# Expert weights in seven 1 MB buffers, with products in groups of four loads

## The chip, the cores and the metric

The kernel runs on one NeuronCore of a Trainium2 chip, in one launch. The metric is the device time of the program in microseconds (us), as the median of its runs. TensorE (PE) multiplies matrices, VectorE (DVE), ScalarE (ACT) and GpSimd (POOL) work element by element, and SyncE (SP) issues nearly all transfers from HBM into on-chip memory. Each engine works through its own instructions in a fixed order and waits at semaphores for the others.

## The reference

Two blocks follow each other on 256 tokens of width 1024, all in fp32. The first block has two kinds of attention, a cross attention and a layer of experts; the second has two layers with modulation, feed-forward networks and mixers, and it carries a second stream of 256 context rows beside the tokens. What matters here is the expert layer of the first block:

```python
group_logits = t @ w_group + b_group                 # 4 groups of 8 experts
g_sel = argmax(group_logits); g_w = softmax(group_logits)[g_sel]
top_vals, top_idx = lax.top_k(expert logits of g_sel, 2)
weights = softmax(top_vals) * g_w
# for each of 32 experts, on the tokens sent to it
hb = silu(xb @ w_gate[e]) * (xb @ w_up[e])           # w_gate, w_up: 1024 x 512
out[token] += (hb @ w_down[e]) * weight              # w_down: 512 x 1024
return x + out
```

All 32 experts' weights are read whatever the routing: 32 x 3 x 2 MB is 192 MB of the 617 MB that the program moves. The context stream of the second block does not depend on the first block, so its work can be done at any time before the tokens need it.

## The kernel before

Two instruction streams are woven into one program. The stream *fore* (tiles named f...) does the first block, the experts (`moe`) and then the tokens of the second block. The stream *back* (tiles b...) does the context rows: `late` and `context` give its parts. A scheduler merges both at build time into one fixed order per engine. It goes by priorities, a start and a slope per section in the table `SEG`, and by its own model of when each instruction can start. On each engine a stream's instructions keep their own order (`link`).

A weight load of fore is one transfer of 128 x 2048 fp32, 1 MB, into a buffer of the tag `raw`, of which fore has 4; a load of back is 128 x 1024, 512 KB, into one of 5. All of them are issued by SP in one order (`load`): a load waits until the last reader of its buffer is done, and everything behind it on SP waits too. For most products ACT rounds the weights (tile `sph`), POOL for back or DVE for fore takes the rest (`spl`), and PE multiplies both parts; a back buffer comes free when POOL is done with it. Expert weights go to PE as they are, so an expert buffer comes free when PE has finished its products.

The experts are worked off in eight groups of four experts. `experts_in` goes over 8 chunks of the model width: per chunk it issues two loads, one of gate and one of up weights, and then multiplies the up load and the gate load, four products of 32 columns each, one per expert. `experts_out` does the same with 4 x 2 loads of the down weights. So a group of experts takes 24 loads, in pairs, and all eight take 192. After the fifth group `spill` handles one more block of 32 tokens with six loads in the same four buffers. A loop for further spills follows the last group; in this run it is not entered. `gather` brings the tokens of the next two groups, `combine` adds results to the residual. Behind `moe` the token stage of the second block begins.

Of the kernel before, what the change touches and what calls it, by code (L numbers as in the profile page):

```python
# [20 lines left out]
KC = 8  # L21
# [18 lines left out]
class X2:  # L40


    def __init__(self, h, l, both=None):
        self.h, self.l, self.both = h, l, both
# [27 lines left out]
class Stream:  # L72
    def __init__(self, K, es, name, bufs, ps_bufs, unit):
        self.K, self.name, self.bufs = K, name, bufs
        self.pool = es.enter_context(K.tc.tile_pool(name=name, bufs=1))
        self.pp = es.enter_context(K.tc.tile_pool(name=name + "p", bufs=ps_bufs, space=PSUM))
        self.n = self.ada = self.lows = 0
        self.sq = None
        self.pool_low = LOW.get(name)
        self.unit = unit  # L80
        self.chain, self.side = {}, {}
        self.seg(0, 1)

    def seg(self, start, slope):

        self.start, self.slope, self.done = start, slope, 0.0
# [8 lines left out]

    def t(self, tag, shape, dt=F32):
        self.n += 1
        return self.pool.tile(shape, dt, tag=tag, bufs=self.bufs[tag], name=f"{self.name}{tag}{self.n}")

    def parts(self, n=T):  # L100

# [56 lines left out]
class Kern:  # L158
    def __init__(self, tc, I, dbg=None):
        self.tc, self.real, self.I, self.dbg = tc, tc.nc, I, dbg  # L160
        self.nc = Engines(self, tc.nc)
        self.cur = self.stream = None
        self.p0 = tc.cur_priority
        self.after = {}

    def link(self, key, r):
        if self.cur is None:
            return
        for prev in (self.cur.get(key), self.after.pop(key, None)):
            if prev is None:  # L170
                continue
            self.tc.add_manual_dep(
                r.ins, prev, mybir.DependencyInfo(mybir.DependencyClass.NoSync, mybir.DependencyReason.DATA),
                reason="stream order")
        self.cur[key] = r.ins.name
# [20 lines left out]
    def pair(self, S, src):  # L196

        if S.unit == 2048:
            raw = self.load(S, src)
            return raw[:, :1024], raw[:, 1024:]  # L200
        return [self.load(S, src[:, i * 1024:(i + 1) * 1024]) for i in range(2)]

    def misc(self, S, tag, shape, src, dt=F32):
        t = S.t(tag, shape, dt)
        self.real.gpsimd.dma_start(t, src)
        return t
# [824 lines left out]
    def moe(self, S):  # L1031
# [7 lines left out]
        xx = S.t("xx", [128, 2, 2, 1024], F32R)  # L1039
# [12 lines left out]
        def ct(n):  # L1052
            used[0] += n
            return scratch[:, used[0] - n:used[0]]
# [23 lines left out]
        dg = ct(8).rearrange("p (b n) -> p b n", b=2)  # L1078
# [58 lines left out]
        def onehot(base, n, b, shift=None):  # L1137
            d = S.t("c", [128, 2])
            if shift is None:
                ts(d, dest[:, :, b], -float(base), None, op0=OP.add)  # L1140
            else:
                tt(d, dest[:, :, b], shift.to_broadcast([128, 2]), op=OP.subtract)
            o, f = S.t("k1", [128, n], F32R), S.t("k1", [128, n])
            ts(f, iota[:, :n], d[:, 0:1], None, op0=OP.is_equal)
            stt(o, iota[:, :n], d[:, 1:2], f, op0=OP.is_equal, op1=OP.add)
            return o
# [13 lines left out]
        def combine(py, s):  # L1160

            o, ws = s
            Yh, Yl = S.t("k4", [128, 1024], F32R), S.t("k4", [128, 1024], F32R)
            for i in range(2):
                q = slice(i * 512, (i + 1) * 512)
                self.split_to(Yh[:, q], Yl[:, q], py[i], ws)
            for d in range(0, KC, 2):
                p = S.ps([128, 2, T])
                for i in range(2):
                    q = slice((d + i) * 128, (d + i + 1) * 128)  # L1170
                    self.mm(p[:, i], Yh[:, q], o, True, False)
                    self.mm(p[:, i], Yl[:, q], o, False, True)
                nc.vector.tensor_tensor(xres[:, d:d + 2], xres[:, d:d + 2], p, op=OP.add)

        wg, wu, wd = I["w_eg"], I["w_eu"], I["w_ed"]

        def gather(pair):
            P = [onehot(256 * pair, 256, b) for b in range(2)]
            xg = [S.t("k4", [128, 4, T]) for _ in range(2)]
            for k in range(0, KC, 2):  # L1180
                p = S.ps([128, 2, T])
                for i in range(2):
                    q = slice((k + i) * 128, (k + i + 1) * 128)
                    for b in range(2):
                        self.mm(p[:, i], hm[b][0][:, q], P[b], b == 0, False)
                        self.mm(p[:, i], hm[b][1][:, q], P[b], False, b == 1)
                nc.scalar.activation(xg[k // 4][:, k % 4:k % 4 + 2], p, AF.Copy)
            return xg

        def experts_in(grp, xg):  # L1190
            g = grp % 2
            pg = [S.ps([128, 512]) for _ in range(2)]
            for k in range(KC):
                raws = [self.load(S, wt[grp, k]) for wt in (wg, wu)]
                for s in (1, 0):
                    for j in range(4):
                        self.mm(pg[s][32 * j:32 * j + 32],
                                xg[k // 4][:, k % 4, g * 128 + 32 * j:g * 128 + 32 * j + 32],
                                raws[s][:, j * 512:(j + 1) * 512], k == 0, k == KC - 1)
            a = self.gated(S, pg[0], 512)  # L1200
            stt(a, a, 0.5, pg[1], op0=OP.mult, op1=OP.mult)
            return a

        def experts_out(grp, a):
            pt = S.ps([128, 512])
            for c in range(4):
                nc.tensor.transpose(pt[:, c * 128:(c + 1) * 128], a[:, c * 128:(c + 1) * 128], self.ident)
            hT = S.t("k2", [128, 4, 128])
            nc.scalar.activation(hT.rearrange("p a b -> p (a b)"), pt, AF.Copy)
            py = [S.ps([128, 512]) for _ in range(2)]  # L1210
            for c in range(4):
                raws = [self.load(S, wd[grp, 2 * c + i]) for i in range(2)]
                for i in (1, 0):
                    for j in range(4):
                        self.mm(py[i][32 * j:32 * j + 32], hT[:, c, 32 * j:32 * j + 32],
                                raws[i][:, j * 512:(j + 1) * 512], c == 0, c == 3)
            slot = S.t("c", [128, 1])
            ts(slot, self.cst[:, C_PCOL:C_PCOL + 1], 128.0 * grp, None, op0=OP.add)
            combine(py, scatter(slot))

        xg = gather(0)

        ta, tb = S.t("k2", [128, 16, 32]), S.t("k2", [128, 16, 32])
# [69 lines left out]
        for grp in range(8):  # L1293
            a = experts_in(grp, xg)
            if grp % 2 == 1 and grp < 7:
                xg = gather(grp // 2 + 1)
            experts_out(grp, a)
            if grp == SPILL:
                spill(sync.value_load(ti[0:1, 0:1], min_val=0, max_val=7),
                      sync.value_load(ti[0:1, 16:17], min_val=0, max_val=3))  # L1300

        self.moe_load = S.chain["sync"]

        n_more = self.real.values_load(ti[0:1, 32:33], min_val=0, max_val=15)
        keep_chain, self.cur = self.cur, None
        with tc.For_i(0, n_more) as it:
# [516 lines left out]


SPILL = 4
DEFER = 0
PLAN = {-1: 'rrr', 0: 'r', 6: 'r', 8: 'raak'}
PLAN_N = 32
CUT = ((0, 9, 9, 9, 9), (0, 3, 3, 3, 3))
FORE = dict(raw=4, sph=3, spl=3, xx=1, k1=6, k2=4, k4=6, c=16, q1=4, dg=2, ld=1, dst=6, wg=2, gc=5, c72=1, rope=1)  # L1830
BACK = dict(raw=5, sph=3, spl=3, xh=1, xl=1, k1=4, k2=4, k4=3, c=16, q1=2, wg=1, gc=4, c72=1)
SEG = dict(c1b=(1150, 2), first=(-5000, 1), ada=(0, 0), c0a=(300, 1.25), c0b=(530, 1.3), c0c=(680, 1.3), ada1=(950, 3), c1a=(1050, 4.8),
           route=(-5000, 1), moe=(365, 2.6), tok=(1050, 1.38))
# [3 lines left out]
def kernel(ctx: ExitStack, tc: tile.TileContext, I, out, dbg=None, stop=None):  # L1837
    K = Kern(tc, I, dbg)
    nc = K.nc
    fore = Stream(K, ctx, "f", FORE, 5, 2048)  # L1840
    back = Stream(K, ctx, "b", BACK, 3, 1024)
    K.dram = ctx.enter_context(tc.tile_pool(name="dram", bufs=1, space=bass.MemoryType.DRAM))
    K.setup(fore, ctx)

    def context():
# [113 lines left out]
    for c in range(KC):  # L1959
        nc.vector.scalar_tensor_tensor(x[:, c], x[:, c], K.gains[:, 5, c:c + 1], bc, op0=OP.mult, op1=OP.mult)  # L1960
        nc.sync.dma_start(out[:, c], x[:, c])


def _units(w):
# [145 lines left out]
```

## Time and profile before

| what | value |
|---|---|
| runs before | 2565.53, 2560.94, 2565.24 us; median 2565.24 |
| profiled execution | 2558.79 us, of which the trace spans 2557.0 |
| TensorE busy over the span | 2373.3 us, 93% |
| VectorE, ScalarE, GpSimd busy | 1533.7, 1228.0, 730.0 us |
| mean granted TensorE clock | 0.964 of full speed |
| moved from and to HBM | 617.23 MB, mean 241 GB/s |

TensorE carries nearly the whole span, and the rest is off its path on average. But the average hides stages with other limits: the expert stage, from the first expert product at 451.7 us to the last at 1306.3 us, has the transfers busy for nine tenths of the time and the other stages for about half. The rows further down are read by stage. A line number does not tell instructions apart here, because all are recorded at line 60 (the helper `Eng`); tile names do.

### The profile page before, as it was taken

To read this page: it belongs to the slowest core of one execution; us is meant where nothing else is said; L and a number is where in the kernel's file an instruction comes from. 1 tells how busy PE (TensorE), PEld (TensorE's weight loads), DVE (VectorE), ACT (ScalarE), POOL (GpSimd) and SP (SyncE) were. 2 spreads that over 40 slices of the span, in tenths; PEclk is the share of its full clock that TensorE was granted. 3 is DMA by queue.
4 is the path that set the end of the run, shared out by engine and by line. 5 is a ranking of instruction groups with operands and counts; after the bars stand their busy time and mean duration, and the time that the engine had idled before them with its cause. 6 is when DMAs were issued, how large, how long until landed. Compare 5 with 4: busy or idle time off the path is not lost. (4 is left out here: it accounts for less than half of the span.)

```text
span 2557.0 us, 46079 instructions
## 1 busy us (share of the span) xinstructions
PE 2373.3 (93%) x17688; PEld 1998.3 (78%) x17688; DVE 1533.7 (60%) x3347; ACT 1228.0 (48%) x2510; POOL 730.0 (29%) x584
## 2 busy tenths in 40 slices
PE   6999998998989999999679999998999899798998
PEld 4767998785666888878348998988899799667897
DVE  6546677235543333352148776767878777677777
ACT  4434554343433433343035555545556555565554
POOL 1000245664524665656141004231000100524000
PEclk9999998999989999999889999999999999899999
DMA  9896543997979898989884554462455355355452
GB/s 373 312 333 255 179 154 132 357 354 293 383 293 364 334 352 306 366 327 343 348 309 168 182 188 142 176 212 103 166 188 191 135 194 182 115 184 197 168 193 102
DMA packets 115231, 617.23 MB, mean 241 GB/s; under 512 B 13232, under 2 KB 14704, under 8 KB 63936
## 3 DMA queue, kind: packets, MB, share of 16 engines
q1 hardware_dynamic: 113616, 610.20, 64.4%
q0 software_dynamic: 1392, 4.06, 0.5%
q8 instruction: 140, 2.29, 0.3%
q14 instruction: 83, 0.68, 0.1%
HBM read 612.11 MB, written 2.10 MB: 240 GB/s over the span
## 5 line engine op out<-in xcount | busy, mean ns | idle before, releaser
L60 POOL TENSOR_TENSOR bspl<-braw,bsph 128x512 fp32r<-128x512 f32 x468 | 608.6, 1309 | 883.3 <-ACT bsph L60 830.4
L60 PE MATMUL fps<-fxx,fsph 128*128 128x512 f32 (+2 forms) x2656 | 734.8, 346 | 19.5 <-DVE fxx L60 10.3
L60 ACT ACTIVATE fsph<-fraw 128x512 fp32r<-128x512 f32 x764 | 479.4, 629 | 483.2 <-PE fps L60 427.9
L60 DVE TENSOR_TENSOR fspl<-fraw,fsph 128x512 fp32r<-128x512 f32 x712 | 498.6, 703 | 234.0 <-ACT fsph L60 216.7
L60 PE MATMUL fps<-fxx,fspl 128*128 128x256 f32 (+1 forms) x2000 | 571.6, 286 | 1.9 <-DVE fspl L60 1.5
L60 PEld LDWEIGHTS fps<-fxx,fsph 128*128 128x128 f32 x2656 | 467.1, 193 | 88.8 <-DVE fxx L60 16.5
L60 ACT ACTIVATE bsph<-braw 128x512 fp32r<-128x512 f32 x468 | 290.9, 629 | 389.9 <-PE bps L60 321.2
L60 PEld LDWEIGHTS fps<-fxx,fspl 128*128 128x128 f32 x2000 | 384.1, 192 | 7.5 <-DVE fspl L60 4.4
L60 PE MATMUL bps<-bxh,bsph 128*128 128x256 f32 x1264 | 363.9, 288 | 5.6 <-ACT bsph L60 3.8
L60 PE MATMUL bps<-bxh,bspl 128*128 128x256 f32 x1264 | 363.7, 288 | 4.2 <-POOL bspl L60 4.0
L60 PE MATMUL bps<-bxl,bsph 128*128 128x256 f32 x1264 | 360.5, 285 | 2.3 <-DVE fk L60 2.2
L60 PE MATMUL fps<-fk,fsph 128*128 128x256 f32 x1632 | 297.8, 284 | 0.0
L60 PEld LDWEIGHTS bps<-bxh,bsph 128*128 128x128 f32 x1264 | 243.5, 193 | 30.6 <-issue 11.9
L60 PEld LDWEIGHTS bps<-bxh,bspl 128*128 128x128 f32 x1264 | 243.1, 192 | 24.6 <-POOL bspl L60 17.3
L60 PEld LDWEIGHTS fps<-fk,fsph 128*128 128x128 f32 x1632 | 254.7, 192 | 3.8 <-issue 0.9
L60 PEld LDWEIGHTS bps<-bxl,bsph 128*128 128x128 f32 x1264 | 243.3, 192 | 10.7 <-issue 8.1
L60 POOL TENSOR_TENSOR fk<-fk,fk 128x512 f32<-128x512 f32 x16 | 21.2, 1323 | 774.2 <-ACT fk L60 769.1
L60 PE MATMUL fps<-fraw,fk 128*32 128x512 f32 (+1 forms) x1600 | 211.2, 642 | 29.9 <-DMA fraw<-in_w_eu_dram 17.9
L60 PE MATMUL fps<-fk,fspl 128*128 128x256 f32 x816 | 230.8, 283 | 0.0
L60 DVE SCALAR_TENSOR_TENSOR bk<-bk,bps 128x256 f32<-128x256 f32 (+1 forms) x148 | 60.3, 411 | 246.9 <-ACT bk L60 244.9
L60 PE MATMUL bps<-bk,bsph 128*128 128x256 f32 x1056 | 198.9, 287 | 3.7 <-DVE bk L60 1.9
L60 PEld LDWEIGHTS bps<-bk,bsph 128*128 128x128 f32 x1056 | 167.6, 194 | 14.0 <-issue 5.9
(351 smaller groups left out, 3203.4 us busy)
## 6 DMA issues: line engine op xcount, KB each, us to landing
fraw<-in_ffn_in_dram SPq DMA_DIRECT2D x88, 1024.0 KB, 4.8
braw<-in_ffn_in_dram SPq DMA_DIRECT2D x132, 512.0 KB, 5.9
fraw<-in_w_eg_dram SPq DMA_DIRECT2D x66, 1024.0 KB, 7.2
fraw<-in_w_eu_dram SPq DMA_DIRECT2D x66, 1024.0 KB, 9.2
fraw<-in_w_ed_dram SPq DMA_DIRECT2D x66, 1024.0 KB, 6.9
fraw<-in_ffn_out_dram SPq DMA_DIRECT2D x44, 1024.0 KB, 4.8
braw<-in_ffn_out_dram SPq DMA_DIRECT2D x66, 512.0 KB, 5.8
braw<-in_ada_w_dram SPq DMA_DIRECT2D x59, 512.0 KB, 7.4
```

What stands on the lines that cost most here:

```text
L60: r = f(*args, **kw)
```

## The change

Three more buffers of 1 MB, tag `more`, serve the experts. Their room comes from tiles that the expert layer does not use (the split tiles `sph` and `spl`, `q1`, `dg`, `ld`, `rope`, `wg`), which now live in a second pool that is closed and opened by `phase`: "f1" for the first block, "fm" with `more` for the experts, "f2" for the rest. `expert` numbers the experts' loads and sends four of each seven to `raw` and three to `more`. The spill still loads into `raw` alone. And products are made for four loads at a time (two chunks), beginning with the load that was issued last; before it was two.

```diff
+    def expert(self, S, src):
+        raw = S.t("raw" if self.experts % 7 < 4 else "more", [128, S.unit])
+        self.experts += 1
+        self.nc.sync.dma_start(raw, src)
+        return raw
...
-            for k in range(KC):
-                raws = [self.load(S, wt[grp, k]) for wt in (wg, wu)]
-                for s in (1, 0):
+            for k0 in range(0, KC, 2):
+                raws = [(k, s, self.expert(S, wt[grp, k])) for k in (k0, k0 + 1) for s, wt in enumerate((wg, wu))]
+                for k, s, raw in reversed(raws):
...
-            for c in range(4):
-                raws = [self.load(S, wd[grp, 2 * c + i]) for i in range(2)]
-                for i in (1, 0):
+            for c0 in (0, 2):
+                raws = [(c, i, self.expert(S, wd[grp, 2 * c + i])) for c in (c0, c0 + 1) for i in range(2)]
+                for c, i, raw in reversed(raws):
...
+        S.phase("fm", ("more",))
         xg = gather(0)
...
+        S.phase("f2", PHASE)
         n_more = self.real.values_load(ti[0:1, 32:33], min_val=0, max_val=15)
...
+PHASE = ("sph", "spl", "q1", "dg", "ld", "rope", "wg")
```

The scheduler weaves both streams anew, and that moves instructions far from the edited lines. Three places are shown, of before and of the change. The number behind a name is the tile's.

TensorE, the end of the seventh group of experts in before; `fps<-fraw,fk 32x512` are the products of one expert load, `fk,fk` belong to `combine`, `bps` is the back stream:

```order
L60 MATMUL bps_8911<-bk_8636,bsph_8924 128x256 x2
L60 MATMUL bps_8911<-bk_8636,bspl_8925 128x256
L60 MATMUL fps_13906<-fraw_13921,fk_13903 32x512 x4
L60 MATMUL fps_13905<-fraw_13919,fk_13903 32x512 x4
L60 MATMUL fps_13906<-fraw_13933,fk_13903 32x512 x4
L60 MATMUL fps_13905<-fraw_13931,fk_13903 32x512 x4
L60 MATMUL fps_13906<-fraw_13945,fk_13903 32x512 x4
L60 MATMUL fps_13905<-fraw_13943,fk_13903 32x512 x4
L60 MATMUL fps_13973<-fk_13962,fk_13967 128x256
L60 MATMUL fps_13973<-fk_13962,fk_13968 128x256
```

The first row on fraw here belongs to the first of the last 30 expert loads, and from it to the last of them before has no row of back.

TensorE, the start of the eighth group in the change:

```order
L60 MATMUL bps_7957<-bk_7791,bsph_7953 128x256 x2
L60 MATMUL bps_7957<-bk_7791,bspl_7954 128x256
L60 MATMUL bps_7976<-bk_7791,bsph_7972 128x256 x2
L60 MATMUL fps_14005<-fraw_14012,fk_13661 32x512 x4
L60 MATMUL fps_14004<-fraw_14010,fk_13661 32x512 x4
L60 MATMUL fps_14005<-fraw_14008,fk_13661 32x512 x4
L60 MATMUL fps_14004<-fraw_14006,fk_13661 32x512 x4
L60 MATMUL bps_7976<-bk_7791,bspl_7973 128x256
L60 MATMUL bps_7976<-bk_7791,bsph_7972 128x256 x2
L60 MATMUL bps_7976<-bk_7791,bspl_7973 128x256
L60 MATMUL bps_7976<-bk_7791,bsph_7972 128x256 x2
```

Four loads' products stand together, the last load's first, and back's rows go on before and behind them. Counted in the order, between the products of the load ahead of the last 30 and those of the very last one stand 691 matmuls of back in the change, and 72 in before.

SyncE, down loads of the fifth group in before (fraw: expert weights; braw: back's weights):

```order
L60 DMA fraw_13293<-in_w_ed_dram 128x2048
L60 DMA fraw_13295<-in_w_ed_dram 128x2048
L60 DMA braw_6347<-in_ffn_in_dram 128x1024
L60 DMA braw_6422<-in_ffn_in_dram 128x1024
L60 DMA braw_6424<-in_ffn_in_dram 128x1024
L60 DMA fraw_13305<-in_w_ed_dram 128x2048
L60 DMA fraw_13307<-in_w_ed_dram 128x2048
L60 DMA braw_6500<-in_ffn_in_dram 128x1024
L60 DMA braw_6502<-in_ffn_in_dram 128x1024
L60 DMA fraw_13317<-in_w_ed_dram 128x2048
```

Here two expert loads alternate with two or three of back's.

SyncE, gate and up loads of the sixth group in the change:

```order
L60 DMA fraw_13552<-in_w_eg_dram 128x2048
L60 DMA fmore_13554<-in_w_eu_dram 128x2048
L60 DMA fmore_13572<-in_w_eg_dram 128x2048
L60 DMA fmore_13574<-in_w_eu_dram 128x2048
L60 DMA fraw_13576<-in_w_eg_dram 128x2048
L60 DMA braw_6202<-in_ffn_out_dram 128x1024
L60 DMA braw_6274<-in_ffn_out_dram 128x1024
L60 DMA braw_6276<-in_ffn_out_dram 128x1024
L60 DMA fraw_13578<-in_w_eu_dram 128x2048
L60 DMA fraw_13596<-in_w_eg_dram 128x2048
```

Four expert loads now come one behind the other, with three or four of back's between such fours.

SyncE ahead of the expert stage, before, at the fourth expert load (`fraw_12269`):

```order
L60 DMA braw_1558<-in_ffn_out_dram 128x1024
L60 DMA braw_1560<-in_ffn_out_dram 128x1024
L60 DMA braw_1632<-in_ffn_in_dram 128x1024
L60 DMA fraw_12269<-in_w_eu_dram 128x2048
L60 DMA braw_1634<-in_ffn_in_dram 128x1024
```

The same place in the change, where the fourth load is `fraw_12268`:

```order
L60 DMA braw_1563<-in_ffn_out_dram 128x1024
L60 DMA fraw_12268<-in_w_eu_dram 128x2048
L60 DMA fmore_12286<-in_w_eg_dram 128x2048
L60 DMA fmore_12288<-in_w_eu_dram 128x2048
L60 DMA fmore_12290<-in_w_eg_dram 128x2048
L60 DMA braw_1635<-in_ffn_in_dram 128x1024
L60 DMA braw_1637<-in_ffn_in_dram 128x1024
```

The fifth to seventh expert loads now stand here, ahead of back's loads that followed the fourth.

## Rows read from the trace of the kernel before

**Rows 1.** Windows: bounds, length, busy us (count) of PE, PEld, DVE, ACT, POOL, clock, DMA, GB/s

```profile
451.70:1228.70 777.00, 741.12 (x5801) 586.54 (x5801) 302.05 (x669) 311.46 (x594) 439.04 (x344) 0.97 0.89 339
1228.70:1306.30 77.60, 45.38 (x262) 11.63 (x261) 8.19 (x18) 4.24 (x7) 1.33 (x2) 0.76 0.95 375
...
1250.00:1300.00 50.00, 26.07 (x152) 5.08 (x148) 3.16 (x10) 1.19 (x2) 0.00 (x0) 0.80 0.98 393
```

**Rows 2.** The same windows, of the instructions on fraw alone

```profile
451.70:1228.70 777.00, 168.04 (x1346) 36.61 (x1347) 0.00 (x0) 0.00 (x0) 0.00 (x0) 0.97 0.89 339
1228.70:1306.30 77.60, 40.70 (x240) 7.60 (x240) 0.00 (x0) 0.00 (x0) 0.00 (x0) 0.76 0.95 375
```

**Rows 3.** Waits of PE in 1228.7:1306.3: us in total, times, longest

```profile
PE fps L60 <- DMA fraw<-in_w_eu_dram: 17.6, 7, 3.8
PE fps L60 <- DMA fraw<-in_w_ed_dram: 10.7, 4, 4.8
```

**Rows 4.** Timeline of PE: start, us, what, idle before and its releaser

```profile
1204.78 0.28 PE L60 MATMUL bps<-bxl,bsph 128*128 128x256 f32 x1
1204.90 0.28 PE L60 MATMUL bps<-bxh,bspl 128*128 128x256 f32 x1
...
1209.79 1.92 PE L60 MATMUL fps<-fraw,fk 128*32 128x512 f32 x16
...
1254.23 1.92 PE L60 MATMUL fps<-fraw,fk 128*32 128x512 f32 x16 [3.41 <-DMA fraw<-in_w_eu_dram]
1259.29 3.62 PE L60 MATMUL fps<-fraw,fk 128*32 128x512 f32 x16 [3.14 <-DMA fraw<-in_w_eu_dram]
```

**Rows 5.** Timeline of SP's queue: the last expert loads

```profile
1202.43 5.45 SPq L60 DMA_DIRECT2D braw<-in_ffn_out_dram  x3
1210.91 20.09 SPq L60 DMA_DIRECT2D fraw<-in_w_ed_dram  x6
...
1275.36 20.17 SPq L60 DMA_DIRECT2D fraw<-in_w_ed_dram  x8
```

**Rows 6.** Waits of PE in 451.7:1228.7

```profile
PE bps L60 <- DVE bk L60: 13.8, 10, 2.9
PE bps L60 <- ACT bk L60: 11.7, 10, 3.0
```

**Rows 7.** The DMA view of 451.7:1306.3, its total

```profile
DMA packets 54797, 292.85 MB, mean 343 GB/s; under 512 B 5871, under 2 KB 5871, under 8 KB 30661
```

**Rows 8.** Windows of the first and the third group of experts

```profile
451.70:548.50 96.80, 96.48 (x798) 78.04 (x797) 27.28 (x53) 38.14 (x69) 64.82 (x51) 1.00 0.96 371
...
658.50:761.70 103.20, 91.68 (x648) 67.18 (x647) 42.87 (x119) 42.82 (x91) 42.35 (x35) 0.92 0.85 329
```

**Rows 9.** PE on fsph in 330:460: count, min/median/max ns, first and last start

```profile
L60 PE MATMUL fps<-fk,fsph x64: 279/283/386, 342.4 to 387.3; 128*128 128x256 f32 x64
```

**Rows 10.** Timeline of SP's queue at the fourth expert load

```profile
384.92 0.33 SPq L60 DMA_DIRECT2D fraw<-in_w_eu_dram  x1
```

**Rows 11.** Windows ahead of and behind the expert stage

```profile
1306.30:2557.00 1250.70, 1178.39 (x8246) 1056.02 (x8242) 939.67 (x1979) 706.90 (x1452) 197.90 (x157) 0.97 0.48 171
...
0.00:451.70 451.70, 408.39 (x3388) 344.10 (x3388) 283.81 (x682) 205.42 (x457) 91.78 (x83) 0.97 0.67 246
```

**Rows 12.** Waits of SP's queue in 451.7:1228.7

```profile
SPq L60 <- POOL bspl L60: 368.7, 132, 11.0
SPq L60 <- PE fps L60: 238.0, 146, 12.6
```

**Rows 13.** DMA issues in 451.7:1306.3: count, KB, us to landing

```profile
fraw<-in_w_eu_dram SPq DMA_DIRECT2D x64, 1024.0 KB, 9.2
braw<-in_ffn_in_dram SPq DMA_DIRECT2D x90, 512.0 KB, 7.1
```

**Rows 14.** The two longest waits of ACT for bsph in 451.7:1228.7

```profile
ACT bsph L60 <- PE bps L60: 267.9, 223, 4.6
...
ACT bsph L60 <- issue: 21.6, 23, 3.6
```

More of the change, by code (lines that the diff above doesn't have):

```diff
@@ L77, in __init__ @@
         self.n = self.ada = self.lows = 0
-        self.sq = None
+        self.sq = self.scope = self.extra = None
+        self.tags = ()
         self.pool_low = LOW.get(name)
@@ L82, in __init__, with phase @@
         self.seg(0, 1)
+    def phase(self, name, tags=()):
+        if self.scope:
+            self.scope.close()
+        self.scope, self.tags = ExitStack(), tags
+        self.extra = self.scope.enter_context(self.K.tc.tile_pool(name=name, bufs=1, side="right", reuse_waits="tile"))
     def seg(self, start, slope):
@@ L97, in t @@
         self.n += 1
-        return self.pool.tile(shape, dt, tag=tag, bufs=self.bufs[tag], name=f"{self.name}{tag}{self.n}")
+        pool = self.extra if tag in self.tags else self.pool
+        return pool.tile(shape, dt, tag=tag, bufs=self.bufs[tag], name=f"{self.name}{tag}{self.n}")
     def parts(self, n=T):
@@ L164, in __init__ @@
         self.after = {}
+        self.experts = 0
     def link(self, key, r):
@@ L1198, in experts_in @@
                                 xg[k // 4][:, k % 4, g * 128 + 32 * j:g * 128 + 32 * j + 32],
-                                raws[s][:, j * 512:(j + 1) * 512], k == 0, k == KC - 1)
+                                raw[:, j * 512:(j + 1) * 512], k == 1, k == KC - 2)
             a = self.gated(S, pg[0], 512)
@@ L1210, in experts_out @@
             py = [S.ps([128, 512]) for _ in range(2)]
-            for c in range(4):
-                raws = [self.load(S, wd[grp, 2 * c + i]) for i in range(2)]
-                for i in (1, 0):
+            for c0 in (0, 2):
+                raws = [(c, i, self.expert(S, wd[grp, 2 * c + i])) for c in (c0, c0 + 1) for i in range(2)]
+                for c, i, raw in reversed(raws):
                     for j in range(4):
                         self.mm(py[i][32 * j:32 * j + 32], hT[:, c, 32 * j:32 * j + 32],
-                                raws[i][:, j * 512:(j + 1) * 512], c == 0, c == 3)
+                                raw[:, j * 512:(j + 1) * 512], c == 1, c == 2)
             slot = S.t("c", [128, 1])
@@ L1829 @@
 CUT = ((0, 9, 9, 9, 9), (0, 3, 3, 3, 3))
-FORE = dict(raw=4, sph=3, spl=3, xx=1, k1=6, k2=4, k4=6, c=16, q1=4, dg=2, ld=1, dst=6, wg=2, gc=5, c72=1, rope=1)
+FORE = dict(raw=4, sph=3, spl=3, xx=1, k1=6, k2=4, k4=6, c=16, q1=4, dg=2, ld=1, dst=6, wg=2, gc=5, c72=1, rope=1, more=3)
 BACK = dict(raw=5, sph=3, spl=3, xh=1, xl=1, k1=4, k2=4, k4=3, c=16, q1=2, wg=1, gc=4, c72=1)
@@ L1842 @@
     K.dram = ctx.enter_context(tc.tile_pool(name="dram", bufs=1, space=bass.MemoryType.DRAM))
+    fore.phase("f1", PHASE)
     K.setup(fore, ctx)
@@ L1961 @@
         nc.sync.dma_start(out[:, c], x[:, c])
+    fore.scope.close()
 def _units(w):
```

## Prediction, made blind

> **What bounds the kernel now.** The page's average (TensorE 93% busy) says that only TensorE counts. The windows show an exception [rows 1]. From 451.7 to 1228.7 us, with experts and back's work side by side, PE is busy for 741.12 of 777.0 us, and DMA for 0.89. From there to the last expert product at 1306.3 us it is the other way round: PE is busy for 45.38 of 77.6 us at a clock of 0.76, DMA for 0.95, and POOL, which works for back alone, stands nearly still. The waits of PE say on what: 17.6 and 10.7 us on expert weights [rows 3]. The queue of SP says why: after the loads of 1202 us it issues expert weights alone [rows 5]. Back's share of the stage is used up, and 30 expert loads are left with nothing beside them. In the 50 us from 1250 us they come at 393 GB/s.
>
> The timeline shows the second price of this tail [rows 4]. Two loads' products took 1.92 us in the midst of back's work; in the tail they are each time preceded by a wait of some 3 us, and often take 3.62 us, which is the half clock. Summed: 240 products took 40.70 us, against 168.04 us for 1346 ahead of it [rows 2], so 170 against 125 ns each.
>
> So the stage has a part that TensorE sets and a part that transfers set, one behind the other. I read from the order of the changed kernel that they are laid over each other: 691 of back's matmuls now stand where 72 stood.
>
> **The sum, step by step.** All against the profiled execution, 2558.79 us, which is 6.45 us below the median of the runs.
>
> First, the tail. If back's work covers the waits, its 240 products cost 240 x 125 ns = 30.0 us, and its 22 other matmuls what they cost now (45.38 - 40.70 = 4.7 us). The rest of the stage keeps its 777.0 us. That makes 811.7 for 854.6 us: **-42.9**.
>
> Second, back's work by count. In the order before, back has 1097 matmuls ahead of the first expert product, 4075 up to the last and 1181 behind it; now 1063, 4039 and 1251. The 70 that go behind the stage run at 0.12 us apart [rows 4]; that part has PE busy for 1178.39 of 1250.7 us [rows 11], so they count in full: +8.4. The 36 fewer in the stage cost (777.0 - 168.0)/4075 = 0.149 us each, waits and the little else of fore included: -5.4. Ahead of the stage PE is idle for 43 of 451.7 us [rows 11], so that 34 fewer bring between 0 and 4 us; I take -2. Together **+1**.
>
> Third, whether the transfers keep up. The stage moves 292.85 MB [rows 7]. In 822 us (the result below) this is 356 GB/s on the mean. The kernel held 371 over the 96.8 us of the first group of experts, but 329 in the third [rows 8], and 393 in the tail. But the work must match locally, too. At 393 GB/s a 1 MB load costs 2.67 us and one of back's half of it. By the new order of SP, the third group has 24 expert loads and 18 of back's, 88 us; the fourth 24 and 9, 76 us. For PE they have 375 and 290 of back's matmuls: 56 + 24 = 80 us and 43 + 24 = 67 us, at 0.149 us a matmul and 1 us a load (eight products). There 8 and 9 us are short. In the other six PE needs as much or more: 101 against 96 us in the second, 121 against 96 in the sixth. The seven buffers let transfers run ahead by at most 7 x 2.67 = 18.7 us, and how much of it is there when the third group begins the trace can't show. So between 0 and 17; I take half: **+8**.
>
> Fourth, the end. PE has four loads' products behind the last landing instead of two: 2 x 1 us, **+2**.
>
> Fifth, the start. Loads five to seven need room that `sph` and others hold. Its last reader is done at 387.3 us [rows 9], and SP stands at the fourth load at 384.92 us [rows 10], so they wait 2 or 3 us and land long before 451.7 us. That hides behind PE's work on back, whose loads come behind them; uncovered it would cost their 8 us of transfer once. It gives 8 us of transfers back to the stage, which the third step counts within its lead. I take **0**.
>
> Sixth, a group of four begins with its last load, and this load goes into the buffer of the first load of the four before, whose products come last. So it can be issued only when those four are done: at the earliest 2.67 us and a latency later it is there, and never before. As a bound the landing of an up load is 9.2 us now, queue included [rows 13]. Between two fours stand mostly 60 to 120 of back's matmuls, 7 to 14 us. In fours that follow at once it shows as a wait of up to 9 us; without back's work it is no loss either, since three loads of the next four are under way meanwhile (8 us). I take **0**, with 0 to 10 us for the few close pairs.
>
> The sum is -42.9 + 1 + 8 + 2 = -32 us: 2527 for a profiled execution, and with 6.45 us more **2533 us** for the median. Its own range by the ends of these terms, with 10 us for the waits of back that get another neighbour [rows 6], is 2510 to 2552.
>
> **A rule that speaks against it.** SP's queue is where back could suffer. The trace shows 7.1 us from issue to landing for back's loads of 512 KB, of which their own transfer is 1.3 us [rows 13]. The Trainium skill says (DMA: Bandwidth & Descriptors, Queues, rings and completion order) that the descriptors of one ring are taken up in the order in which they were put there. By that rule a load of back behind four expert loads starts up to 10.7 us late instead of 5.3 us behind two. The trace agrees as far as 7.1 us goes, and no run here shows four in a row beside back's work yet. By the rule the sum holds only as long as back's five buffers cover it; the other result is the second rival below.
>
> **The rivals.** (1) *The transfers give no more than they did.* SP issues in one order, and of its waits 368.7 us go to POOL, which frees back's buffers, against 238.0 us to PE, which frees the experts' [rows 12]. While SP stands at a load of back, no expert load goes out, however many buffers there are. If the rate of the first 777 us, 339 GB/s, were all, 292.85 MB less the 3 MB fetched ahead would take 855 us, as now: 2560 to 2570, within 0.2% (5 us, about what a measurement of this kernel can tell from no change) or little faster. Against it: PE sets the pace in these 777 us, its waits for weights there are not among the large ones [rows 6], and DMA was at 0.89, not at its end.
>
> (2) *Slower: back's loads come late behind bursts of four.* The place is SP's queue in all 48 fours. The cover is large now: the two longest waits of ACT for `bsph` are on PE and on nothing [rows 14], so the weights are there first. Five buffers hold 5 x 24 matmuls of 0.12 us, 14 us, against 10.7 + 1.3 us of queue and transfer plus what SP stands still. If in each four one load of back came late by its own transfer, 48 x 1.34 = 64 us would be lost: -32 + 64 = +32, some 2597. It decides from 32/48 = 0.7 us per four on.
>
> (3) *A larger gain.* If the lead covers the third step in full, and the groups in the middle, at a clock of 0.92 in the third [rows 8], lose a third of their idle time because PE finds weights ready: -32 - 8 - 15 = -55, some 2510, down to 2495.
>
> The Trainium skill has a figure against this last one: the HBM side gives some 358 GB/s per core (DMA: Bandwidth & Descriptors, Where 436 GB/s comes from). An estimate by it is 292.85 MB / 358 = 818 us for the stage, and no gain beyond some 37 us. The trace shows 393 GB/s over 50 us [rows 1], so the figure does not bind this kernel.
>
> **How the numbers follow.** The forecast 0.64; rival 1 0.13, of which 0.04 would still be faster by over 0.2%; rival 2 0.11; rival 3 0.12. Faster: 0.64 + 0.04 + 0.12 = 0.80; within 0.2%: 0.09; slower: 0.11. The predicted time is the forecast's. The range goes from 2498, most of rival 3, to 2568, rival 1, and leaves out rival 2 and what lies below.
>
> **What would show it.** In the profile after, the stage from the first to the last expert product should be 815 to 830 us long, with no stretch of 50 us in which POOL does nothing and PE is half idle. PE's waits on expert weights should be under 20 us instead of the 28 of its tail. The clock from 1200 to 1300 us should be above 0.95. DMA should run at 350 GB/s or more over the stage; if it stays at 339, rival 1 is right. If ACT waits for `braw`, or PE for `bsph` by more than a few us, it is rival 2. The part behind the stage should be longer by 8 us, no more. The prediction is wrong in kind if the tail is gone and the time is not, and in size if the third or the fourth group takes over 100 us.

## The result

| kernel | median of runs | lowest to highest | ratio to before, 95% |
|---|---|---|---|
| before | 2565.39 us (4 runs) | 2560.94 to 2567.00 | |
| changed | 2534.75 us (4 runs) | 2533.22 to 2539.97 | 0.9887 [0.9872, 0.9902] |

The change saves 30.6 us by the medians; the forecast was 2533. The profiled executions stand 25.6 us apart: 2533.22 us (span 2531.4) against 2558.79 (span 2557.0). Split at the first and the last expert product:

| us | ahead of the experts | expert stage | behind it |
|---|---|---|---|
| before [rows 1, 11] | 451.7 | 854.6 | 1250.7 |
| changed | 440.8 | 822.7 | 1267.9 |
| difference | -10.9 | -31.9 | +17.2 |

### The profile page after: what moved, and what is told of

It reads as the page before. It is cut to its first block, busy times and chain, and to the rows that moved or that the text cites. A ratio compares the mean times of both kernels' runs of the same rounds, so it can differ in the third digit from the quotient of the medians.

```text
span 2531.4 us, 46033 instructions
## 1 busy us (share of the span) xinstructions
PE 2348.4 (93%) x17688; PEld 1999.8 (79%) x17688; DVE 1538.3 (61%) x3347; ACT 1228.9 (49%) x2510; POOL 732.8 (29%) x584
## 5 line engine op out<-in xcount | busy, mean ns | idle before, releaser
L60 PE MATMUL bps<-bxh,bsph 128*128 128x256 f32 x1264 | 367.4, 291 | 10.9 <-ACT bsph L60 7.7
L60 PE MATMUL bps<-bxh,bspl 128*128 128x256 f32 x1264 | 369.2, 292 | 7.4 <-POOL bspl L60 7.4
L60 PE MATMUL fps<-fk,fsph 128*128 128x256 f32 x1632 | 290.9, 280 | 0.0
L60 PEld LDWEIGHTS bps<-bxh,bspl 128*128 128x128 f32 x1264 | 248.2, 196 | 30.3 <-issue 20.1
L60 PEld LDWEIGHTS fps<-fk,fsph 128*128 128x128 f32 x1632 | 249.5, 188 | 4.1 <-issue 2.5
L60 PE MATMUL bps<-bk,bspl 128*128 128x256 f32 x528 | 153.4, 291 | 3.6 <-ACT fk L60 2.2
## 6 DMA issues: line engine op xcount, KB each, us to landing
fraw<-in_w_ed_dram SPq DMA_DIRECT2D x39, 1024.0 KB, 10.4
```

What stands on the lines that cost most here:

```text
L60: r = f(*args, **kw)
```

## The profile after

Windows of the changed kernel: bounds, length, busy us (count) of PE, PEld, DVE, ACT, POOL, granted clock, DMA share, GB/s.

```profile
0.00:440.80 440.80, 397.37 (x3356) 336.28 (x3356) 282.83 (x677) 202.59 (x452) 88.47 (x79) 0.96 0.69 257
440.80:1263.50 822.70, 768.08 (x6023) 604.05 (x6022) 302.52 (x685) 315.17 (x600) 439.40 (x344) 0.96 0.89 353
1263.50:2531.40 1267.90, 1182.95 (x8320) 1059.46 (x8312) 952.96 (x1985) 711.12 (x1458) 204.92 (x162) 0.96 0.47 168
...
1200.00:1263.50 63.50, 61.06 (x512) 49.84 (x510) 20.25 (x38) 24.57 (x46) 42.72 (x34) 1.00 0.85 324
1200.00:1300.00 100.00, 90.40 (x722) 77.56 (x721) 47.88 (x85) 41.77 (x77) 62.49 (x50) 0.97 0.74 284
```

The tail is gone. In the last 63.5 us of the stage PE is busy for 61.06 us at the full clock, POOL (which works for back) for 42.72, and DMA stands at 0.85; before, the last 77.6 us had PE busy for 45.38 at 0.76 and POOL for 1.33 [rows 1].

The stage's own row on the expert products alone, first `fraw`, then `fmore` (the second answer leaves out engines without work):

```profile
440.80:1263.50 822.70, 114.81 (x936) 28.12 (x936) 0.00 (x0) 0.00 (x0) 0.00 (x0) 0.96 0.89 353
440.80:1263.50 822.70, 81.50 (x648) 19.76 (x648) 0.96 0.89 353
```

Products of both tags run beside each other at times, and the two rows then count that time twice, 6.9 us in all. Counted once, the 1584 records (two to a product) take 189.4 us, 120 ns each; before it was 208.7 [rows 2], where one tag serves all.

What PE waits for in the stage, us in total, times, longest:

```profile
PE bps L60 <- DVE bk L60: 23.4, 14, 3.9
PE bps L60 <- ACT bk L60: 8.7, 13, 1.2
PE bps L60 <- POOL bspl L60: 7.5, 10, 0.8
PE bps L60 <- ACT bsph L60: 4.4, 4, 1.2
...
PE fps L60 <- DMA fraw<-in_w_eu_dram: 1.6, 1, 1.6
```

28.3 us of waits on weights [rows 3] have become one of 1.6. What PE waits for now is inside back: its DVE results for 23.4 us instead of 13.8 [rows 6].

The DMA view of the stage, its total and back's commonest load (count, KB, median us from issue to landing), then ACT's one wait for back's weights and SP's longest wait:

```profile
DMA packets 54648, 290.45 MB, mean 353 GB/s; under 512 B 5845, under 2 KB 5940, under 8 KB 30896
...
braw<-in_ffn_in_dram SPq DMA_DIRECT2D x90, 512.0 KB, 7.4
```

```profile
ACT bsph L60 <- DMA braw<-in_ffn_in_dram: 5.3, 1, 5.3
```

```profile
SPq L60 <- POOL bspl L60: 493.4, 163, 14.4
```

The stage moves nearly what it moved [rows 7], at 353 instead of 343 GB/s. The median landing of back's commonest load hardly changed, 7.4 us for 7.1 [rows 13], but it mixes loads behind a four with loads behind nothing. Taken one by one, 35 of back's 168 loads in the stage were issued with four expert loads still under way, and they landed after 11.2 us (median; 15.3 at the longest). With two under way it was 7.3 us, and 7.2 before. One of the 35, first SP's queue and then the time to landing of the load in its last row:

```profile
442.90 0.42 SPq L60 DMA_DIRECT2D fraw<-in_w_eu_dram  x1
443.37 0.42 SPq L60 DMA_DIRECT2D fraw<-in_w_eg_dram  x1
443.84 0.63 SPq L60 DMA_DIRECT2D fraw<-in_w_eu_dram  x1
444.57 0.69 SPq L60 DMA_DIRECT2D fraw<-in_w_eg_dram  x1
449.25 0.33 SPq L60 DMA_DIRECT2D braw<-in_ffn_in_dram  x1
```

```profile
DMA to landing us min/median/max: 10.0/10.0/10.0
```

So a four does delay the load behind it, by some 4 us against a pair. It costs little here because the load comes early enough: ACT waited for back's weights once.

Behind the stage, PE's largest wait, in the change and in before:

```profile
PE fps L60 <- DVE fk L60: 44.9, 18, 5.1
```

```profile
PE fps L60 <- DVE fk L60: 35.3, 18, 3.9
```

The 1267.9 us hold 4.6 us more of PE work than the 1250.7 of before and 12.6 us more of idle time [rows 11].

## The experiments

The theory: the tail is what costs; back's work runs out 30 loads before the experts end, and the change gains by leaving back's rows for the end. The rivals: the buffers gain (more transfers in flight), the fours gain (fewer switches of PE), or the new pools do. One count serves throughout: back's matmuls on PE in the built order, ahead of the first expert product, beside the experts and behind the last one, as in the prediction's second step.

**Seven buffers without the fours** (`seven_pairs`).

```diff
-            for k0 in range(0, KC, 2):
-                raws = [(k, s, self.expert(S, wt[grp, k])) for k in (k0, k0 + 1) for s, wt in enumerate((wg, wu))]
+            for k0 in range(KC):
+                raws = [(k0, s, self.expert(S, wt[grp, k0])) for s, wt in enumerate((wg, wu))]
...
```

The down loads are changed in the same way.

> The change without its fours: seven buffers, products in pairs as before. In its order back has only 3340 matmuls inside the expert stage (4039 in the change), none of the stage is left without back, and 1950 stand behind it (1251). Theory (what counts is that back's work lies beside the loads; TensorE and the transfers both must be fed): inside, PE needs 3340 x 0.149 + 198 = 696 us, the transfers 261 loads of 1 MB x 2.67 = 697 us; some 730 us with their mutual waits, 92 less than the change, and 699 x 0.12 = 84 us more behind it: 2527, from 2510 to 2545. Rival (the fours bring the gain, the buffers alone do not): 2555 to 2570, as before.

Measured: 2529.77 us (2526.26 to 2535.30), ratio 0.9873 [0.9837, 0.9908]. Its stage and what lies behind:

```profile
439.80:1178.40 738.60, 691.31 (x5323) 513.35 (x5322) 256.57 (x608) 267.12 (x512) 363.53 (x287) 0.97 0.93 372
1178.40:2526.43 1348.03, 1268.38 (x9020) 1146.70 (x9012) 1009.01 (x2063) 755.43 (x1546) 282.01 (x220) 0.97 0.49 170
```

The experts end 85 us sooner than in the change, because only 3340 of back's matmuls stand beside them; the others stand behind, where this kernel takes 80 us more than the change: +97.3 us over before for 769 rows, 0.127 us each. The time is the change's or less. So the fours save nothing in the total, though they do in PE's products (196.6 us here, counted once, against 189.4), and it hardly matters how early the experts end. The stage also held 372 GB/s for 738.6 us, which ends the first rival (339 at most). The Trainium skill's figure of some 358 GB/s on the HBM side (DMA: Bandwidth & Descriptors, Where 436 GB/s comes from), weighed in the prediction, did not bind here.

**Fours with the first load first** (`fours_forward`).

```diff
-                for k, s, raw in reversed(raws):
+                for k, s, raw in raws:
...
```

> The change with the products of a group of four in the order of the loads, first load first. In its order back has 3060 matmuls inside the expert stage and 2230 behind it. Theory: the stage is then set by the transfers, 255 loads of 1 MB x 2.67 = 681 us and some 25 us of waits, 705 to 730 us, and 979 x 0.12 = 117 us more lie behind it: 2538, from 2525 to 2555. Rival (to begin with the last load matters in itself, since PE then never stops within a four): over 2560, with PE's waits on expert weights above 40 us.

Measured: 2569.50 us (2564.51 to 2573.79), ratio 1.0015 [0.9999, 1.0032]. A miss for the theory, and the rival has only the number: no wait on weights is among the seven largest of its stage (the seventh is 2.4 us). The timeline of PE shows what it is instead:

```profile
922.95 1.04 PE L60 MATMUL fps<-fmore,fk 128*32 128x512 f32 x2
923.93 0.38 PE L60 MATMUL bps<-bxh,bspl 128*128 128x256 f32 x1
...
927.57 0.38 PE L60 MATMUL bps<-bxl,bsph 128*128 128x256 f32 x1
927.89 1.06 PE L60 MATMUL fps<-fmore,fk 128*32 128x512 f32 x6
```

The same place in the change reads

```profile
1171.97 0.40 PE L60 MATMUL bps<-bk,bsph 128*128 128x256 f32 x2
1172.30 3.64 PE L60 MATMUL fps<-fraw,fk 128*32 128x512 f32 x32
1175.87 0.39 PE L60 MATMUL bps<-bk,bspl 128*128 128x256 f32 x1
```

In the built order the four loads of a group no longer stand together. The change has 48 stretches of sixteen products without a row of back between them; here 3 are left, 117 stretches hold four products (mostly one load's), and in 19 of the 198 loads back's rows stand even between the load's own four. One product alone takes 1.04 us, three together 1.06, four 1.07 (the median of such stretches), the sixteen of a four 3.64. The products took 235.9 us (144.78 on `fraw`, 96.53 on `fmore`, less what overlaps) instead of 189.4: 46 us, more than the 35 by which this kernel is slower than the change. That the scheduler splits the groups when the load that lands first is multiplied first is read from the order; why its model does so was not tried.

**The order inside a four** (`strip_order`): the products of one column strip (one expert) directly behind each other; the sums are the same.

```diff
-                for k, s, raw in reversed(raws):
-                    for j in range(4):
+                for j in range(4):
+                    for k, s, raw in reversed(raws):
...
```

> The change with only the order of the 16 products inside a four turned: first the four loads' products of the first expert, then of the second and so on, where the change takes the four experts of one load in succession. Bytes, buffers, counts and the place between back's work stay. In the trace of fours_forward two records alone (one product) took 1.04 us and eight in succession 1.06 us. Theory (products of 32 columns run beside each other only if they go to different column strips and stand next to each other): a four takes several times its 3.64 us, at least 16 x 0.5 = 8 us, so 50 x 4 to 50 x 10 us more: 2730 to 3050. Rival (the order within a four does not matter, fours_forward was slow for another reason): 2525 to 2545.

Measured: 2746.33 us (2 runs), ratio 1.0700 [1.0665, 1.0734].

```profile
439.50:1489.00 1049.50, 1007.51 (x6037) 665.60 (x6037) 291.01 (x685) 316.18 (x602) 439.13 (x345) 0.98 0.72 277
```

```profile
498.13 1.90 PE L60 MATMUL fps<-fraw,fk 128*32 128x512 f32 x4
499.87 0.59 PE L60 MATMUL fps<-fmore,fk 128*32 128x512 f32 x1
499.88 0.62 PE L60 MATMUL fps<-fraw,fk 128*32 128x512 f32 x1
500.30 0.59 PE L60 MATMUL fps<-fmore,fk 128*32 128x512 f32 x1
500.33 0.59 PE L60 MATMUL fps<-fraw,fk 128*32 128x512 f32 x1
500.73 0.59 PE L60 MATMUL fps<-fmore,fk 128*32 128x512 f32 x1
...
505.11 1.88 PE L60 MATMUL fps<-fmore,fk 128*32 128x512 f32 x4
```

Each strip has four records on `fraw` and then four on `fmore`. The first strip's four on `fraw` stand alone, four in 1.90 us; then come pairs, the later half of one strip beside the earlier half of the next; the last strip's four on `fmore` stand alone again. So records of one strip start 0.43 us apart, and the 32 of this four take 8.9 us; in the change 32 take 3.64 us, 0.11 us each. The granted clock is 1.00 at both places. PE is busy for 239 us more in the stage (1007.5 against 768.1). So 32-column products of different strips that stand next to each other overlap, those of the same strip don't. That successive products of a strip go to two result tiles in turn does not help them; whether it is the strip of the array or that of the result that they share can't be told apart here, since both go together. This is the mechanism of the miss above, shown by itself.

**The fours alone, with four buffers** (`fours_four`): before, with only the loops of the change.

> The kernel before with the fours alone: four buffers, groups of four, last load first. In its order no back matmul stands behind the 168th load, 72 in before. Theory: the tail of 30 loads stays, and as a four fills all buffers, each four there waits for its loads from the start: 10.7 us of loads, some 3 us of latency and 4 us of products, 17 us for 7.5 fours instead of 10.7; some 45 us slower than before, 2590 to 2625. Rival (fours let PE work in longer stretches and bring the gain): under 2555.

Measured: 2618.79 us (2617.11 to 2621.84), ratio 1.0216 [1.0183, 1.0250]. PE's first waits in its stage of 903.7 us:

```profile
PE fps L60 <- DMA fraw<-in_w_eu_dram: 39.1, 6, 10.4
PE fps L60 <- DMA fraw<-in_w_ed_dram: 32.8, 4, 10.1
```

With four buffers the next four cannot start loading before this one is done, and the wait is the four's own landing, 10 us at the longest. The three buffers are what makes the fours bearable.

**The pools alone** (`phase_only`): the second pool is opened and closed, four buffers, pairs.

```diff
-        raw = S.t("raw" if self.experts % 7 < 4 else "more", [128, S.unit])
+        raw = S.t("raw", [128, S.unit])
...
```

> The change's pools in phases, but four buffers and pairs as before: only the placement of tiles differs. Theory: the tail of 30 loads without back stays (144 back matmuls there, 72 in before), so the stage is as long as before, 845 to 860 us. But it starts some 11 us earlier, as in the change, if that comes from the pools, which gives the 34 matmuls behind the stage some of it back: 2555 to 2565. Rival (the pools themselves bring the change's gain): 2530 to 2540.

Measured: 2554.60 us (10 runs, 2550.83 to 2558.28), ratio 0.9966 [0.9949, 0.9982]. That is at the lower edge of what was expected and far from the rival. Some 11 us come with the pools, that is, from the other places of the tiles and the order that the scheduler then builds. The experts begin at 437.7 us, 14 us sooner than before; the stage takes 866.4 us, and the tail is there (waits on `w_eu` of 18.5 us).

**The order alone** (`spread_four`): before with nothing new but one rule for the scheduler: back may be at most 42 matmuls further on after each pair of expert loads.

```diff
+        i = SPREAD[0] + self.pairs_done * SPREAD[1]
+        self.tc.add_manual_dep(
+            self.back_mm[i].ins, self.last_mm.ins.name,
+            mybir.DependencyInfo(mybir.DependencyClass.NoSync, mybir.DependencyReason.DATA), reason="spread")
...
+SPREAD = (1100, 42)
```

> The kernel before, with its four buffers, pairs and pools, and only an order of its own: behind each pair of loads a matmul of back may at the earliest be the 42nd further on, so back's work reaches into what was the tail. Between the 168th and the last load stand 719 of back's matmuls (before 72, the change 691). Theory A (the gain is the order; buffers only got the scheduler to make it): the tail's 43 us go, less some 10 us of waits, as loads are asked for two pairs ahead at most: 2535 to 2552. Theory B (without the larger lead PE waits for weights at each pair, by 0.5 us or more at 99 pairs): 2560 to 2600, with PE's waits on expert weights above 40 us.

Measured: 2526.76 us (2523.94 to 2529.31), ratio 0.9843 [0.9813, 0.9873].

```profile
447.60:1273.20 825.60, 783.33 (x6040) 599.26 (x6040) 315.41 (x687) 318.02 (x601) 441.10 (x345) 0.96 0.92 355
```

No buffer, no pool, no four, and a stage of 825.6 us at 355 GB/s. It gains more than the change, and more than I expected. No wait of PE on weights is among its seven largest (the seventh is 0.8 us). This shows the tail by itself: with the same four buffers, moving back's rows is enough.

**Five and six buffers, pairs** (`five_pairs`, `six_pairs`): as `seven_pairs`, with `% 5` and one more buffer, `% 6` and two.

> Pools in phases, pairs, and one more buffer instead of three. In its order back has 4109 matmuls in the expert stage as in the pools-only kernel, but 454 of them behind the 168th load (144 there), and none behind the 192nd. Theory A (the order is the gain): the stage goes from 866 to some 830 us, the rest stays: 2527, from 2518 to 2542. Theory B (each buffer brings its part of the lead): 2543 to 2552, a third of the way from 2554.6 with four to 2529.8 with seven.

> The same with two more buffers. In its order back has 3557 matmuls in the stage (seven buffers 3340, five 4109) and 1733 behind it. Theory A: matmuls of back cost nearly the same inside and behind, so the time is that of seven pairs: 2530, from 2520 to 2542. Theory B (each buffer brings its part): 2535 to 2545, above five by order and below four.

Measured: five 2542.71 us (2538.47 to 2543.50), ratio 0.9910 [0.9881, 0.9939]; six 2521.83 us (2518.41 to 2522.42), ratio 0.9824 [0.9795, 0.9854]. Six:

```profile
438.90:1204.60 765.70, 716.15 (x5542) 538.27 (x5541) 268.15 (x651) 281.08 (x543) 381.52 (x301) 0.97 0.93 366
```

Six pairs beat the change, and seven pairs too, with no overlap of the runs. That fits the expectation of theory A and not that of B: the time does not fall with each buffer. PE still waits for weights with five (14.7 us in three entries); with six such waits are not among the seven largest. Five lies at the edge between both expectations and tells nothing apart.

**Seven buffers, with the experts held back** (`paced_seven`): pairs, but a pair's products may stand only when back has come 42 matmuls further, so that back has 4039 rows in the stage, as in the change.

```diff
+            self.tc.add_manual_dep(
+                r.ins, self.back_mm[self.paced].ins.name,
+                mybir.DependencyInfo(mybir.DependencyClass.NoSync, mybir.DependencyReason.DATA), reason="pace")
...
+PACE = (1050, 42)
```

> Seven buffers and pairs, and a pair's products may start only when back has got 42 matmuls further on than at the pair before. So back has 4039 matmuls in the stage and 1251 behind it, to the matmul as in the change, but evenly over the eight groups and with pairs between. Theory A (what counts is how much of back lies beside the loads, not the fours): as the change, 2535, from 2522 to 2545, and the stage 810 to 830 us long. Rival (fours save PE something at each group): over 2548.

Measured: 2576.77 us (2574.01 to 2582.17), ratio 1.0049 [1.0031, 1.0067]. A miss, and not for the rival's reason either, since `seven_pairs` without any fours is at 2530. Its stage and two windows of it:

```profile
440.20:1305.70 865.50, 795.99 (x6024) 606.29 (x6023) 299.37 (x685) 314.01 (x600) 438.75 (x345) 0.94 0.86 335
640.00:740.00 100.00, 82.27 (x551) 61.65 (x549) 43.28 (x114) 40.95 (x86) 43.02 (x35) 0.88 0.75 279
740.00:840.00 100.00, 86.17 (x580) 64.18 (x581) 27.39 (x81) 33.14 (x68) 37.15 (x31) 0.85 0.65 247
```

and the same two windows of the change:

```profile
640.00:740.00 100.00, 88.97 (x619) 65.46 (x615) 49.26 (x122) 40.83 (x88) 38.88 (x32) 0.88 0.90 354
740.00:840.00 100.00, 87.58 (x686) 64.62 (x678) 34.20 (x106) 35.91 (x72) 39.27 (x31) 0.94 0.89 357
```

Here back itself waits for ACT and DVE between its rows (15.7 and 12.7 us in these 200 us; 6.7 and 13.6 in the change). The built order of the change puts experts there (375 and 290 of back's rows in the third and fourth group); the rule forbids it (518 and 508), so PE stands idle for 31.6 of the 200 us instead of 23.5, and DMA falls to 0.75 and 0.65. Idle time is not all of it: over the stage it is 14.9 us more than in the change, and PE's busy time is 27.9 us more for nearly as many records, at a clock of 0.94 instead of 0.96 and with products of 200.3 us, counted once, instead of 189.4. `spread_four` holds back the filler, this one holds back the work that should be filled: nearly as many rows in the stage (4055 and 4039), 50 us apart, though the two differ in buffers and pools as well.

**Pools and order together** (`spread_phase`): `phase_only` with the rule of `spread_four`, the count starting at 1066 instead of 1100.

> The pools-only kernel (four buffers, pairs, pools in phases) with the spread order of spread_four. If the two gains are independent, the pools' 11 us and the order's 37 us against before add up: 2518, from 2510 to 2524, with a stage of 820 to 835 us that starts at 440 us. If the pools' 11 us are a matter of how that one order fell, not of the pools: 2524 to 2532, as spread_four.

Measured: 2522.83 us (2513.49 to 2529.12), ratio 0.9819 [0.9794, 0.9844]. The median lies where both gains would add up, but its runs reach over nearly all of those of `spread_four`; whether the 11 us of the pools come on top is not settled.

## Why the prediction was right, step by step

- **The tail is what costs, and the change covers it: right.** `spread_four` shows it without any other edit. For the stage the prediction has 822 us, which is 854.6 less the whole sum; by its own terms alone (-42.9, -5.4, +8, +2) it is 816.3. Measured: 822.7.
- **First step, the products: right in kind, too small.** 125 ns were taken for those of the tail; counted once, all 1584 records now take 120, as a four runs a little tighter than a pair (124 in `seven_pairs`). They save 19.4 us, where 10.7 were in the sum.
- **Second step, by count: the counts were right, the times were not.** In the stage PE's work without the products went from 577.8 to 578.7 us, +0.9 for the -5.4 worked out, though 36 matmuls fewer stand there. Ahead of it -10.9 was measured for -2: PE's idle time stayed at 43 us and its busy time fell by 11.0. Of that, 34 matmuls at 0.12 us are 4 us, and the rest comes with the pools, as every kernel with them starts its experts at 435 to 441 us and the others at 447.6 to 451.7. Which of the moved tiles does it stays open. Behind it +17.2 was measured for +8.4: the rows' work is 4.6 us, but fore's wait for its own DVE chain grew by 9.6 us; the likely reason is that back's rows now stand at other places between its parts, but no run shows it. The count does not set that part's time: `fours_four` has 1181 rows there, as before, and took 1265.3 us. I counted rows and took it that they run as densely there as elsewhere.
- **Third step, transfers short by 8 us: the cause is wrong.** PE's idle time in the stage is 54.6 us where 46 follow from the sum (35.9 outside the tail, +8, +2), and 1.6 us of it is for weights. What took its place is back's own waiting (23.4 us on DVE instead of 13.8). The third group did take longer than its 88 us by transfers, about 100 us, the size that the prediction named as a sign against itself. But PE waited there for back's DVE and ACT and not once for weights, at a clock of 0.88 and with DMA at 0.90 in the window from 640 to 740 us above. Products, other work and idle time were off by -8.7, +6.3 and +8.7 us, which makes the 6.4 us of the stage.
- **Fourth and sixth step, the fours:** with seven buffers the one wait on weights is 1.6 us; `fours_four` shows that the bound of 9 us in the sixth step is real where buffers are missing (10.4 and 10.1 us at the longest).
- **Fifth step, the start of the loads: 0, as taken.** SP issues loads five to seven at 377.70, 378.13 and 378.60 us, right behind the fourth at 375.00.
- **The rivals.** The transfers gave 353 GB/s, and 372 in `seven_pairs`, so the first is out, although SP stood longer at back's loads than before (493.4 us of waits on POOL instead of 368.7 [rows 12]). The second, back's loads late behind fours, had its mechanism right: a load behind four lands some 4 us later than one behind two, 11.2 us after its issue. It had the price wrong, as ACT waited once, 5.3 us. By the rule of the Trainium skill cited there (DMA: Bandwidth & Descriptors, Queues, rings and completion order) descriptors of one ring are taken up in order; the prediction's estimate by it was a start up to 5.4 us later, and the trace agrees with its 4 us. The third, a larger gain, did not come.
- **The range by the terms, 2510 to 2552, does not come out of them.** With 10 us either way for back's waits the ends of the terms are 2513 and 2564. The range that was stated, 2498 to 2568, rests on the rivals and not on this one.

So three terms were off by -8.9, +6.4 and +8.8 us (start, stage, behind), and their sum, 6.3 us, is what lies between the 2527 foreseen for a profiled execution and the 2533.22 that was profiled. That the median is hit within 2 us owes something to chance: the profiled execution of before lay 6.45 us below the median that the prediction had, and the one of the change only 1.5.

And one thing the prediction did not ask: whether the fours are needed. They aren't. Pools 11 us, buffers 25 us more (2554.60 to 2529.77), fours +5 us (2534.75, within the spread of the runs), and the order alone does as much as all of them.

## What to carry to other kernels

Look for the stretch of a stage where its filler has run out (an engine that serves only the filler stands still, the bound engine is half idle), and move the filler there by an ordering rule before buying buffers; hold back the filler rather than the work that it fills (one kernel of each kind was run here). When a change goes through a scheduler, count in the built order what stands ahead of, beside and behind the stage, and look at whether operations that are fast only side by side are still side by side. An equal count does not mean an equal time: `paced_seven` and the change have the same counts and lie 42 us apart.

## What the runs showed of the hardware

- Products of 32 columns (128x512, fp32) on different column strips overlap when adjacent: at a granted clock of 1.00, 0.11 us a record in a run of 32, 1.04 us for a product (two records) alone, and 0.43 us from record to record when products of one strip follow each other. Between two orders of the same products lie 212 us of this kernel.
- The transfers held 372 GB/s over 738.6 us, beside TensorE work that kept PE busy for 691 of them; the prediction had seen 371 over 96.8 us [rows 8] and counted on 356.
- On SP's one queue a 512 KB load landed 11.2 us after its issue with four 1 MB loads still under way ahead of it, and 7.3 with two (medians in the changed kernel).
